# Expert stage of a decoder trunk: weight splits issued one at a time with side jobs between them, few-token experts in 64 packed columns, gates and tail reordered

## The chip, the cores and the metric

The kernel runs on one core of one Trainium2 chip. The metric is the device time of one execution in microseconds; it is taken over several executions and told as their median. TensorE is PE in the profile (its weight loads PEld), VectorE is DVE, ScalarE is ACT, SyncE is SP. SP issues the weight loads.

## The reference, cut to what matters

A trunk of layers for 256 tokens of width 1024 in float32: attention layers with dense feed-forward parts, then a mixture of eight experts, then a last RMS norm. The change touches the experts and the last norm. Each token takes two of eight experts, by the two largest router logits:

```python
logits = (xf @ router).astype(jnp.float32)
top_val, top_idx = lax.top_k(logits, TOP_K)          # TOP_K = 2
gates = jax.nn.softmax(top_val, axis=-1)
...
def swiglu(x, w_gate, w_up, w_down):
    return (jax.nn.silu(x @ w_gate) * (x @ w_up)) @ w_down
...
y_rows = lax.map(expert_block, (x_rows, blk_expert)).reshape(n_rows, dm)
y_rows = y_rows * row_gate[:, None].astype(y_rows.dtype)
y = jax.ops.segment_sum(y_rows, row_tok, num_segments=n + 1)[:n]
...
return rms_norm(x, final_norm)
```

An expert's weights are 1024 x 3584 (gate and up) and 3584 x 1024 (down), 44 MB in float32 for each of the eight.

## The kernel before

Up to about 510 us the attention and dense layers run. The expert stage follows. It has 56 **steps**: eight experts, p0 to p7 in an order by token count, times seven chunks of 512 hidden units. The arm that ran takes p0 to p4 as *few* (at most 64 tokens each, 35 steps) and p5 to p7 as *others* (up to 128 tokens, 21 steps). The two groups are interleaved by the share that each has done, so about five few steps stand beside three others. p0 ends at step 10; the last steps of p0, p5, p1, p2, p6 and p3 have their last down-product two steps later, at steps 12, 19, 23, 34, 37 and 46, inside the stream. p7 and p4 end in the tail.

**Weights.** A step needs six pieces of 128 x 2048 floats (1 MB): two of gate, two of down (for the step two earlier), two of up. SP loads them in order into a ring `raw` of `RAWS = 6` (L944). `fill` (L947) splits a piece in two: ACT copies it rounded into `wH` (L955), DVE writes the rest `wL` (L956); rings of `SPLIT = 4` each. The products use both halves.

**A step** (loop at L1272, `for s in range(n_steps + 1)`), in the order in which it is written, which is kept on PE, ACT and DVE:

- the gate products (`ffn_in`; few: 4 matmuls with `wH`, L1105, and 4 with `wL`, L1110, a piece; others 12, L1107, L1108, L1110), then `fill`, which splits all free pieces, two here;
- the copy g out of PSUM (L1124, ACT);
- `turn` for the step before: its g and u are transposed (few: multiplied with a fold matrix that adds the two halves, L1134; others: L1136); `activate` queues four operations in `later_`: silu (L1143, ACT), product (L1144, DVE), high half (L1145, ACT), low half (L1146, DVE). `fill` pops one of them after each split piece;
- `job(s)`, at most one side job or several, depending on its due step;
- the down products of the step two earlier (`ffn_out`, `y`), `fill` (two pieces), `job(s)`;
- the up products, `fill` (two pieces), the copy u (L1124, ACT).

**Side jobs.** `gather` fetches an expert's tokens by one-hot matmuls (one-hots L1069 on DVE, matmuls L1081, copies L1086 on ACT, then L1090, L1092, the copy of `rs` L1094 on DVE and of `ST` L1095 on ACT); it starts at steps 1, 3, 11, 18, 22, 33 and 36. When an expert has ended, `y_split` (L1165 ACT, L1166 DVE) splits its output and `combine` (L1174 and L1175 on PE, L1178 on DVE) adds it, scaled by the gate, into `xs` in four pieces. They are due two steps after the end and take the place at the head of `jobs`:

```python
for _ in range(min(left, max(1, -(-left // max(2 * (due - s) - 1, 1))))):
    next(j)
    next(j, None)
...
adding = [s + 2, combine(*y_split(y), gateq[:, :, p2:p2 + 1], kept[p2][1]), 4]
```

With one step left this runs all four pieces at the first `job` of the next step. PSUM banks: a ring of two `bA` (g, u, gather, combine) and of two `bT` (turn), and one `y` for each group.

At step 0 `gates()` (L1046 to L1049 and on) and `to_order()` stand ahead of the copy g. In the tail the remaining jobs run, then the activation of the last step, its last products in two halves, two combines and the last norm (L1359).

Of the kernel before, what the change touches and what calls it, by code (L numbers as in the profile page):

```python
# [8 lines left out]
F32 = mybir.dt.float32  # L9
# [3 lines left out]
AF = mybir.ActivationFunctionType  # L13
# [19 lines left out]
SPLIT = 4  # L33
HEAD = 3
# [24 lines left out]
for _n, _w in (("iota", 128), ("fold", 128)):  # L59
    CM[_n] = (_o, _o + _w)  # L60
    _o += _w
# [11 lines left out]
def trunk(tc, I, out):  # L73
    nc = tc.nc
    ctx = ExitStack()
    with ctx:
# [808 lines left out]
        with ExitStack() as ph:  # L885
# [3 lines left out]
            def few_at(a):  # L889

                i = c_m("iota")[:, 0:P // 2]
                return i[:, :, None].to_broadcast([P, P // 2, 2]) if a == 0 else i[:, None, :].to_broadcast([P, 2, P // 2])

            def c_m(n):
                return cm[:, CM[n][0]:CM[n][1]]

# [22 lines left out]
            for a in range(2):  # L919
                d = few_at(a)  # L920
# [10 lines left out]
            class Pieces:  # L931
# [14 lines left out]

                def fill(self, n=SPLIT):  # L947
                    while len(self.ready) < n:
                        self.load(1)
                        if not self.loaded:  # L950
                            break
                        raw = self.loaded.pop(0)
                        w = raw.shape[-1]
                        h, l = wHs.next()[:, :w], wLs.next()[:, :w]
                        nc.scalar.activation(h, raw, AF.Copy)  # L955
                        nc.vector.tensor_tensor(l, raw, h.bitcast(F32), op=ALU.subtract)  # L956
                        self.ready.append((h, l))
                        self.load(RAWS)
                        if later_:
                            later_.pop(0)()  # L960

                def take(self, n):
                    self.fill(n)
# [21 lines left out]
            early.fill()  # L985
# [73 lines left out]
            def onehots(pos, mode):  # L1059
# [3 lines left out]
                for a, S_ in enumerate((Sg, Ss)):  # L1063
                    at = c_m("iota") if mode is False else io[:, a, :] if mode is None else few_at(a)
                    for tt in range(NT):
                        o = S_[:, tt, :]
                        if mode:
                            o = o.rearrange("p (a b) -> p a b", a=at.shape[1])
# [3 lines left out]
            def gather(Sg, Ss, X, ST, rs, first=False):  # L1072


                for h, src in enumerate((hnH, hnL)):
                    for k0 in range(0, KD, 4):
                        pt = bank("T" if first and k0 else "A").rearrange("p (k j) -> p k j", k=4)
                        for k in range(4):
# [430 lines left out]
```

## Time and profile before

| | us |
|---|---|
| median of three runs (lowest, highest) | 1490.66 (1484.51, 1490.75) |
| the profiled execution, device time | 1486.26 |
| its span in the profile | 1484.5 |
| PE busy | 1381.8 (93%) |
| DVE busy | 1182.0 (80%) |
| ACT busy | 1033.0 (70%) |
| read from HBM | 425.61 MB, 287 GB/s over the span |

A line of the timeline reads: start, duration, engine, line of the program, operation, out<-in, form, count, and in brackets the idle time before it and what ended it. A PE matmul's duration is modelled and overlaps the next one; the distance from start to start tells what one takes. An SPq line is the queue of the loads; x2 are the two pieces of one chunk. A line of windows gives the busy time of each engine in that stretch, the granted clock of PE, the busy share of the DMA engines and the rate.

### The profile page before, as it was taken

What the parts mean: (1) busy time and instruction counts of PE and PEld (TensorE: products, weight loads), DVE (VectorE), ACT (ScalarE), POOL (GpSimd) and SP (SyncE); (2) the same over time, 40 slices, a digit from 0 to 9 for tenths busy, and PEclk for the clock granted to TensorE, in tenths of its full rate; (3) what the DMA queues carried; (4) which work ended last, traced back from release to release, by engine and by line L of the source; (5) the groups of instructions that cost most, each with busy time, mean ns of one, the idle gap of its engine ahead of it and who ended that gap; (6) DMA issues with size and microseconds to landing.
All of it is one profiled execution on the core that took longest, in us unless ns stands there. A gap on an engine that the chain in (4) does not pass through costs nothing. (4 is left out here: it accounts for less than half of the span.)

```text
span 1484.5 us, 19753 instructions
## 1 busy us (share of the span) xinstructions
PE 1381.8 (93%) x7351; PEld 1178.0 (79%) x7351; DVE 1182.0 (80%) x1255; ACT 1033.0 (70%) x1050; POOL 2.5 (0%) x12
## 2 busy tenths in 40 slices
PE   8999999999999779999899999999989899989994
PEld 7778999999887668888688777788878778868883
DVE  6847656565674578899889889799987799989995
ACT  6444444444575478898688868698867688868882
POOL 0000000000000000000000000000000000000000
PEclk9999999999999789999999999999999999989998
DMA  8435355442314378999989989799997799989990
GB/s 337 171 117 212 130 196 200 171 161 106 109 63 159 142 260 331 365 420 419 358 320 421 370 302 385 289 422 421 421 381 273 298 396 419 420 326 408 419 385 31
DMA packets 57228, 428.06 MB, mean 288 GB/s; under 512 B 6272, under 2 KB 6656, under 8 KB 10144
## 3 DMA queue, kind: packets, MB, share of 16 engines
q1 hardware_dynamic: 56784, 425.50, 73.2%
q8 instruction: 60, 0.98, 0.3%
q0 software_dynamic: 336, 1.18, 0.2%
q14 instruction: 48, 0.39, 0.1%
HBM read 425.61 MB, written 1.05 MB: 287 GB/s over the span
## 5 line engine op out<-in xcount | busy, mean ns | idle before, releaser
L956 DVE TENSOR_TENSOR wL<-raw,wH 128x2048 fp32r<-128x2048 f32 (+1 forms) x338 | 760.8, 2276 | 92.5 <-ACT wH L955 87.0
L955 ACT ACTIVATE wH<-raw 128x2048 fp32r<-128x2048 f32 (+1 forms) x338 | 634.0, 1900 | 94.9 <-PE y L1108 32.1
L147 ACT ACTIVATE wH<-raw 128x1024 fp32r<-128x1024 f32 (+3 forms) x137 | 142.4, 1042 | 167.6 <-PE pst L202 118.1
L1110 PE MATMUL bA<-wL,X 128*128 128x512 f32 x896 | 245.1, 395 | 0.0
L148 DVE TENSOR_TENSOR wL<-raw,wH 128x1024 fp32r<-128x1024 f32 (+3 forms) x137 | 164.1, 1199 | 86.9 <-ACT wH L147 78.4
L1110 PEld LDWEIGHTS bA<-wL,X 128*128 128x128 f32 x896 | 172.7, 193 | 36.3
L1105 PE MATMUL bA<-wH,X 128*128 128x512 f32 x560 | 157.1, 402 | 10.4 <-ACT g L1124 5.8
L1105 PEld LDWEIGHTS bA<-wH,X 128*128 128x128 f32 x560 | 109.2, 197 | 33.2 <-ACT g L1124 6.2
L1107 PE MATMUL bA<-wH,X 128*128 128x512 f32 x336 | 131.7, 392 | 0.3 <-ACT ST L1095 0.2
L1108 PE MATMUL bA<-wH,X 128*128 128x512 f32 x336 | 130.9, 389 | 0.0
L201 PE MATMUL pst<-hTH,wH 128*128 128x256 f32 x512 | 127.3, 286 | 0.9 <-DVE vC L743 0.5
L202 PE MATMUL pst<-hTL,wH 128*128 128x256 f32 x512 | 127.0, 285 | 0.3
L1110 PE MATMUL y<-wL,a 128*128 128x512 f32 x448 | 126.2, 404 | 0.0
L1110 PEld LDWEIGHTS y<-wL,a 128*128 128x128 f32 x448 | 88.7, 198 | 18.9
L201 PEld LDWEIGHTS pst<-hTH,wH 128*128 128x128 f32 x512 | 98.8, 193 | 2.3 <-DVE vC L743 0.9
L202 PEld LDWEIGHTS pst<-hTL,wH 128*128 128x128 f32 x512 | 99.0, 193 | 0.9 <-DVE hTL L249 0.7
L1105 PE MATMUL y<-wH,a 128*128 128x512 f32 x280 | 84.0, 422 | 6.5 <-DVE a L1146 5.0
L1108 PE MATMUL y<-wH,a 128*128 128x512 f32 x168 | 68.4, 407 | 7.7 <-DVE a L1146 7.7
L1107 PEld LDWEIGHTS bA<-wH,X 128*128 128x128 f32 x336 | 63.1, 188 | 14.2 <-ACT ST L1095 1.2
L1108 PEld LDWEIGHTS bA<-wH,X 128*128 128x128 f32 x336 | 63.1, 188 | 13.0
L204 PE MATMUL pst<-hTH,wL 128*128 128x256 f32 x512 | 72.7, 284 | 0.0
L1105 PEld LDWEIGHTS y<-wH,a 128*128 128x128 f32 x280 | 55.3, 207 | 18.1 <-DVE a L1146 6.2
(290 smaller groups left out, 1815.6 us busy)
## 6 DMA issues: line engine op xcount, KB each, us to landing
raw<-in_m_g SPq DMA_DIRECT2D x112, 1024.0 KB, 7.7
raw<-in_m_u SPq DMA_DIRECT2D x112, 1024.0 KB, 7.3
raw<-in_m_d SPq DMA_DIRECT2D x110, 1024.0 KB, 7.4
raw<-in_f_gu SPq DMA_DIRECT2D x14, 2048.0 KB, 8.5
raw<-in_f_d SPq DMA_DIRECT2D x7, 2048.0 KB, 8.4
raw<-in_w_eo SPq DMA_DIRECT2D x2, 2048.0 KB, 8.4
raw<-in_w_oo SPq DMA_DIRECT2D x2, 2048.0 KB, 7.9
raw<-in_w_qa SPq DMA_DIRECT2D x4, 512.0 KB, 7.6
```

Source lines behind the costliest of these rows:

```text
L147: nc.scalar.activation(h[:, :w], src, AF.Copy)
L148: nc.vector.tensor_tensor(l[:, :w], src, h[:, :w].bitcast(F32), op=ALU.subtract)
L201: ins.append(nc.tensor.matmul(o, a[0], b[0], start=st, stop=False))
L202: ins.append(nc.tensor.matmul(o, a[w], b[1 - w], start=False, stop=False))
L204: ins.append(nc.tensor.matmul(o, a[1 - w], b[w], start=False, stop=sp))
L955: nc.scalar.activation(h, raw, AF.Copy)
L956: nc.vector.tensor_tensor(l, raw, h.bitcast(F32), op=ALU.subtract)
L1105: nc.tensor.matmul(o, both(x), b[0], start=st, stop=False)
L1107: nc.tensor.matmul(o, x[:, 0], b[0], start=st, stop=False)
L1108: nc.tensor.matmul(o, x[:, 1], b[0], start=False, stop=False)
L1110: nc.tensor.matmul(o, both(x) if few_ else x[:, 0], b[1], start=False, stop=sp)
```

## The change

- **Splits singly.** `fill` splits one piece. It is called six times a step, twice after each pair of pieces, with other work between. It takes a function `first` that is run on DVE between the ACT copy and the DVE subtraction. Each `fill` pops one queued activation operation, also when nothing was split; the list has an empty place before the high half.
- **Order of a step.** `turn` and its job now stand behind the gate products, then fill, the copy g, fill; behind the down products a job, fill, `y_split`, fill; behind the up products fill, the copy u, fill. A side job's matmuls are issued at the job, its copy on ACT later, its addition on DVE ahead of the next subtraction (`first`).
- **Combine** is due three steps after the end: one piece, two pieces and one piece at three successive places instead of four at one. `y_split` is one operation of 1024 columns on each engine instead of two of 512.
- **Few tokens in 64 columns.** For p1 to p4 the high and low parts stand side by side in 64 + 64 columns (p0 keeps them interleaved). The fold matrix has 64 columns, the silu, product, high and low operate on 128 x 4 x 64, both transposed halves share one `bT` bank, and a gather has three jobs with two copies instead of five jobs with four copies.
- The copy of `rs` moves from DVE to ACT. `to_order()` moves behind step 0's fills, `gates()` and the ordering of the gates to step 3; `pick` and `picked` get tiles of their own.
- **Tail.** The activation of the last step stands ahead of the down products of the step before; p7's combine stands between the two halves of the last products; the multiplication with the last norm's gain stands ahead of the mean square's root, and the last scaling is split between DVE and ACT.

```diff
-                def fill(self, n=SPLIT):
+                def fill(self, first=None):
+                    if len(self.ready) < SPLIT:
...
                         nc.scalar.activation(h, raw, AF.Copy)
+                            if first is not None:
+                                first()
+                                first = None
                         nc.vector.tensor_tensor(l, raw, h.bitcast(F32), op=ALU.subtract)
...
+                    if first is not None:
+                        first()
+                    if later_:
+                        later_.pop(0)()
...
+                w, n = (HALF, KD) if few_ else (P, 4)
...
+                                nc.tensor.matmul(pt[:, k], src[:, tt, c], Sg[:, tt, 0:w], start=tt == 0, stop=tt == 1)
                         yield
+                        o = X[:, :, 0, h * HALF:(h + 1) * HALF] if few_ else X[:, k0:k0 + n, h, :]
...
-                nc.vector.tensor_copy(rs, pt[:, S:S + 1])
+                nc.scalar.activation(rs, pt[:, S:S + 1], AF.Copy)
...
+                if few_:
+                    tp = bank("T").rearrange("p (a f j) -> p a f j", a=2, f=4)
+                    tps = [tp[:, 0], tp[:, 1]]
...
+                if few_:
+                    s, hi, lo = s[:, :, 0:HALF], a[:, :, 0, 0:HALF], a[:, :, 0, HALF:P]
                 later_.extend((
                     lambda: nc.scalar.activation(s, tps[0], AF.Silu),
                     lambda: nc.vector.tensor_tensor(s, s, tps[1], op=ALU.mult),
+                    lambda: None,
+                    lambda: nc.scalar.activation(hi, s, AF.Copy),
+                    lambda: nc.vector.tensor_tensor(lo, s, hi.bitcast(F32), op=ALU.subtract)))
...
-                def job(s):
+                def job(s, more=False):
+                    due, j, left, dve = jobs[0]
+                    for i in range(min(left, max(1, -(-left // max(due - s, 1)))) if more else 1):
+                        if i > 0:
                             next(j, None)
+                        next(j)
+                        jobs[0][2] -= 1
...
+                    return (copy, None) if dve else (None, copy)
...
-                        if s == 0:
-                            gates()
-                            to_order()
-                        g = scaled(pt, rs, "g")
...
+                    on_dve, on_act = job(s)
+                    ws.fill(on_dve)
+                    g = scaled(pt, rs, "g")
+                    if on_act is not None:
+                        on_act()
+                    ws.fill()
+                    if s == 0:
+                        to_order()
+                    if s == 3:
+                        gates()
+                        in_order(gateq, gate)
...
                         ffn_out(p2 in A, ws, held.pop(("a", s - 2)), y, c2 == 0, c2 == NC - 1)
...
-                        adding = [s + 2, combine(*y_split(y), gateq[:, :, p2:p2 + 1], kept[p2][1]), 4]
+                        on_dve, on_act = job(s, True)
+                        ws.fill(on_dve)
+                        if c2 == NC - 1:
+                            adding = [s + 3, combine(*y_split(y), gateq[:, :, p2:p2 + 1], kept[p2][1]), 4, True]
+                            jobs.insert(0, adding)
+                        if on_act is not None:
+                            on_act()
+                        ws.fill()
+                    pt = ffn_in(mode, ws, X)
+                    ws.fill()
+                    held[s] = (g, scaled(pt, rs, "u"))
+                    ws.fill()
...
-                for j in jobs:
-                    run(j[1])
+                few_ = steps[-1][0] in A
                 settle()
+                a = activate(few_, turn(few_, held.pop(n_steps - 1)))
+                settle()
...
+                ffn_out(p2 in A, ws, held.pop(("a", n_steps - 2)), y, c2 == 0, c2 == NC - 1)
...
+                    for j in jobs:
+                        run(j)
+                    jobs.clear()
+                    parts = y_split(y, slice(n, n + 1), yy)
...
+                for tt in range(NT):
+                    nc.vector.tensor_tensor(of[:, tt, :], xs[:, tt, :], gf, op=ALU.mult)
                 last_rstd()
...
-                        nc.vector.scalar_tensor_tensor(of[:, tt, c], xs[:, tt, c], fr[:, tt:tt + 1], gf[:, c],
-                                                       op0=ALU.mult, op1=ALU.mult)
+                        if tt:
+                            nc.scalar.activation(of[:, tt, c], of[:, tt, c], AF.Copy, scale=fr[:, tt:tt + 1])
+                        else:
+                            nc.vector.tensor_scalar(of[:, tt, c], of[:, tt, c], fr[:, tt:tt + 1], None, op0=ALU.mult)
```

The first end of an expert in the arm that ran is p0's. On DVE, before, from the low half at step 12 on (L956 the split, L1178 the pieces of combine, L1144 the product, L1146 the low half, here of another step):

```order
L1146 TENSOR_TENSOR a_4840<-s_4838,a_4840 128x4x128
L956 TENSOR_TENSOR wL_4829<-raw_4817,wH_4825 128x2048
L956 TENSOR_TENSOR wL_4830<-raw_4818,wH_4826 128x2048
L1178 SCALAR_TENSOR_TENSOR xs<-bA_4832,gateq,xs 128x512
L1178 SCALAR_TENSOR_TENSOR xs<-bA_4831,gateq,xs 128x512
L1178 SCALAR_TENSOR_TENSOR xs<-bA_4832,gateq,xs 128x512
L1178 SCALAR_TENSOR_TENSOR xs<-bA_4831,gateq,xs 128x512
L956 TENSOR_TENSOR wL_4827<-raw_4819,wH_4823 128x2048
L956 TENSOR_TENSOR wL_4828<-raw_4820,wH_4824 128x2048
L1144 TENSOR_TENSOR s_4838<-s_4838,bT_4834 128x512
```

And now at the same place (L957 the split, L1188 the pieces, L1156 the product, L1159 the low half):

```order
L1188 SCALAR_TENSOR_TENSOR xs<-bA_4832,gateq,xs 128x512
L957 TENSOR_TENSOR wL_4829<-raw_4817,wH_4825 128x2048
L957 TENSOR_TENSOR wL_4830<-raw_4818,wH_4826 128x2048
L1156 TENSOR_TENSOR s_4838<-s_4838,bT_4834 128x4x64
L1188 SCALAR_TENSOR_TENSOR xs<-bA_4831,gateq,xs 128x512
L1188 SCALAR_TENSOR_TENSOR xs<-bA_4832,gateq,xs 128x512
L957 TENSOR_TENSOR wL_4827<-raw_4819,wH_4823 128x2048
L957 TENSOR_TENSOR wL_4828<-raw_4820,wH_4824 128x2048
L957 TENSOR_TENSOR wL_4829<-raw_4821,wH_4825 128x2048
L1159 TENSOR_TENSOR a_4839<-s_4838,a_4839 128x4x64
L957 TENSOR_TENSOR wL_4830<-raw_4822,wH_4826 128x2048
L1188 SCALAR_TENSOR_TENSOR xs<-bA_4831,gateq,xs 128x512
```

The four additions stood in one row behind two splits; now they stand one, two and one, each ahead of a split, with six splits, the product and a low half between the first and the last.

On ACT, a step of a few expert without a side job, before (L955 the copy of the split, L1124 the copies g and u, L1143 silu, L1145 the high half):

```order
L955 ACTIVATE wH_4823<-raw_4817 128x2048
L955 ACTIVATE wH_4824<-raw_4818 128x2048
L1124 ACTIVATE g_4835<-bA_4832,rs_4852 128x512
L955 ACTIVATE wH_4825<-raw_4819 128x2048
L1143 ACTIVATE s_4838<-bT_4833 128x512
L955 ACTIVATE wH_4826<-raw_4820 128x2048
L955 ACTIVATE wH_4823<-raw_4821 128x2048
L1145 ACTIVATE a_4840<-s_4838 128x4x128
L955 ACTIVATE wH_4824<-raw_4822 128x2048
L1124 ACTIVATE u_4837<-bA_4831,rs_4852 128x512
```

And now (L953 the copy of the split, L1129 g and u, L1155 silu, L1158 the high half):

```order
L953 ACTIVATE wH_4825<-raw_4817 128x2048
L1155 ACTIVATE s_4838<-bT_4834 128x4x64
L1129 ACTIVATE g_4836<-bA_4831,rs_4853 128x512
L953 ACTIVATE wH_4826<-raw_4818 128x2048
L953 ACTIVATE wH_4823<-raw_4819 128x2048
L953 ACTIVATE wH_4824<-raw_4820 128x2048
L1158 ACTIVATE a_4839<-s_4838 128x4x64
L953 ACTIVATE wH_4825<-raw_4821 128x2048
L1129 ACTIVATE u_4837<-bA_4831,rs_4853 128x512
L953 ACTIVATE wH_4826<-raw_4822 128x2048
```

The copy g stood behind two copies of the split; now it stands behind one of them and the silu, and the copy u stands between two copies of the split as before, with the high half two copies ahead of it.

## Rows read from the trace of the kernel before

**Rows 1.** The queue of the weight loads, the issues of the down pieces of a step (start, duration of the issue): an early pair, the sixth pair after it, two with six steps between them in an even stretch, and the 47th pair after the second row.

```profile
522.19 2.53 SPq L944 DMA_DIRECT2D raw<-in_m_d  x2
...
633.27 2.99 SPq L944 DMA_DIRECT2D raw<-in_m_d  x2
...
1201.69 2.93 SPq L944 DMA_DIRECT2D raw<-in_m_d  x2
...
1291.50 2.93 SPq L944 DMA_DIRECT2D raw<-in_m_d  x2
...
1421.13 2.93 SPq L944 DMA_DIRECT2D raw<-in_m_d  x2
```

**Rows 2.** Busy time of PE, PEld, DVE, ACT, POOL, then PE's granted clock, DMA share and GB/s, in 40 us around p0's end and in 40 us of the even stretch.

```profile
720.00:760.00 40.00, 34.19 (x156) 27.55 (x155) 31.16 (x23) 26.29 (x24) 0.00 (x0) 0.91 0.80 297
1240.00:1280.00 40.00, 39.03 (x190) 32.81 (x189) 38.86 (x23) 34.90 (x27) 0.00 (x0) 1.00 1.01 419
```

**Rows 3.** DVE by line from 633.27 to 1421.13 us: operation and form, count, busy us, mean ns of one, idle time before them and what ended it.

```profile
L956 DVE TENSOR_TENSOR wL<-raw,wH 128x2048 fp32r<-128x2048 f32 x282 | 637.9, 2288 | 62.8 <-ACT wH L955 58.8 <-PE bA L1105 2.2
L1146 DVE TENSOR_TENSOR a<-s,a 128x512 fp32r<-128x512 f32 x47 | 32.2, 685 | 0.0
L1144 DVE TENSOR_TENSOR s<-s,bT 128x512 f32<-128x512 f32 x47 | 32.0, 681 | 0.0
L1178 DVE SCALAR_TENSOR_TENSOR xs<-bA,gateq,xs 128x512 f32<-128x512 f32 x24 | 17.4, 747 | 4.5 <-PE bA L1175 3.9
L1166 DVE TENSOR_TENSOR yy<-y,yy 128x512 fp32r<-128x512 f32 x12 | 8.3, 688 | 4.0 <-ACT yy L1165 4.0
...
L1069 DVE TENSOR_SCALAR Sg<-cm,posq 128x128 fp32r<-128x128 f32 x10 | 2.4, 281 | 0.0
```

**Rows 4.** The timeline of PE in the even stretch: a few step's turn (L1134) and its down products, another expert's products (L1107 on), few products again, the turn of another expert (L1136) and what follows it.

```profile
1219.48 1.05 PE L1134 MATMUL bT<-cm,g 128*128 128x128 f32 x8
1220.37 1.06 PE L1134 MATMUL bT<-cm,u 128*128 128x128 f32 x8
1221.18 1.18 PE L1105 MATMUL y<-wH,a 128*128 128x512 f32 x4
...
1224.99 0.39 PE L1107 MATMUL bA<-wH,X 128*128 128x512 f32 x1
...
1230.44 1.09 PE L1105 MATMUL bA<-wH,X 128*128 128x512 f32 x4
...
1234.17 0.60 PE L1136 MATMUL bT<-cf,g 128*128 128x128 f32 x4
...
1234.98 1.20 PE L1105 MATMUL y<-wH,a 128*128 128x512 f32 x4
```

**Rows 5.** The timeline of PE's weight loads: of a gather (128 columns moved), of the product with one column (L1092), of a fold (128 columns).

```profile
593.09 1.09 PEld L1081 LDWEIGHTS bA<-Sg,hnL 128*128 128x128 f32 x8
...
744.55 0.52 PEld L1092 LDWEIGHTS bA<-ry,Ss 128*128 128x128 f32 x4
...
755.50 0.97 PEld L1134 LDWEIGHTS bT<-cm,u 128*128 128x128 f32 x8
```

**Rows 6.** The timeline at p0's end: DVE's splits, the first combine pieces on PE, and the first split of the next pair.

```profile
731.37 4.48 DVE L956 TENSOR_TENSOR wL<-raw,wH 128x2048 fp32r<-128x2048 f32 x2
...
733.33 0.80 PE L1174 MATMUL bA<-yy,ST 128*128 128x512 f32 x1 [2.55 <-ACT g L1124]
...
736.57 0.79 PE L1174 MATMUL bA<-yy,ST 128*128 128x512 f32 x1 [2.02 <-DVE xs L1178]
...
741.00 1.92 ACT L955 ACTIVATE wH<-raw 128x2048 fp32r<-128x2048 f32 x1 [7.73 <-PE y L1108]
...
742.95 2.29 DVE L956 TENSOR_TENSOR wL<-raw,wH 128x2048 fp32r<-128x2048 f32 x1 [3.52 <-ACT wH L955]
```

**Rows 7.** Stretches of 4 us at and after this end, columns as in the windows above.

```profile
732.00:736.00 4.00, 1.22 (x2) 0.50 (x2) 4.00 (x3) 1.27 (x2) 0.00 (x0) 0.59 1.01 401
740.00:744.00 4.00, 4.00 (x20) 3.29 (x19) 1.05 (x1) 2.62 (x3) 0.00 (x0) 1.00 0.28 115
772.00:776.00 4.00, 4.00 (x18) 3.30 (x18) 4.00 (x3) 4.00 (x5) 0.00 (x0) 1.00 1.01 426
```

**Rows 8.** Waits from 560 to 1460 us: who waits for whom, us in total, times, longest.

```profile
DVE wL L956 <- ACT wH L955: 73.5, 89, 4.6
ACT a L1145 <- DVE s L1144: 44.3, 38, 2.6
```

**Rows 9.** The timeline at step 0: the copy g and the products behind it.

```profile
528.12 0.69 ACT L1124 ACTIVATE g<-bA,rs 128x512 f32<-128x512 f32 x1 [2.42 <-DVE u L1207]
...
528.87 2.08 PE L1105 MATMUL bA<-wH,X 128*128 128x512 f32 x4 [5.81 <-ACT g L1124]
```

**Rows 10.** The timeline of the tail: the last up products, the fold behind the copy u, the down products of the step before the last, the first of the last products, the last norm.

```profile
1446.05 1.09 PE L1110 MATMUL bA<-wL,X 128*128 128x512 f32 x4
...
1450.99 1.16 PE L1134 MATMUL bT<-cm,u 128*128 128x128 f32 x8 [2.96 <-ACT u L1124]
...
1456.72 1.07 PE L1110 MATMUL y<-wL,a 128*128 128x512 f32 x4
...
1464.81 0.73 PE L1105 MATMUL y<-wH,a 128*128 128x512 f32 x2 [1.50 <-DVE a L1146]
...
1478.19 2.74 DVE L1359 SCALAR_TENSOR_TENSOR raw<-xs,fr,gf 128x512 f32<-128x512 f32 x4
```

More of the change, by code (lines that the diff above doesn't have):

```diff
@@ L33 @@
 SPLIT = 4
+HALF = 64
 HEAD = 3
@@ L58 @@
 _o = 0
-for _n, _w in (("iota", 128), ("fold", 128)):
+for _n, _w in (("iota", 128), ("fold", 64)):
     CM[_n] = (_o, _o + _w)
@@ L918, in trunk @@
             io = ss.bufs[0][:, 0:2, :]
-            for a in range(2):
-                d = few_at(a)
+            for a, d in enumerate((half[:, :, None].to_broadcast([P, HALF, 2]), twice)):
                 n = d.shape[1]
@@ L984, in trunk @@
             early.load(RAWS)
-            early.fill()
+            for _ in range(SPLIT):
+                early.fill()
             top = mw.tile([P, NT, 8], F32, name="top")
@@ L1150, in ffn_out, with y_split @@
                 for j, w in enumerate(ws.take(2)):
[L1151 removed]
+                    products([(y[:, n, :], a[:, 2 * j + f], part(w, 2 * f + n), first and j + f == 0,
                                last and j + f == 2) for f in range(2) for n in range(2)], few_)
[L1153 removed]
             ys = []
             for i in range(2):
[L1157 to L1160 removed]
+                ys.append(pa.tile([P, 2, 512], F32, name=f"y{i}"))
+            def y_split(y, n=slice(0, 2), yy=None):
                 if yy is None:
@@ L1314, in experts @@
                     for j, w in enumerate(ws.take(2)):
-                        products([(y[n], a[:, 2 * j + f], part(w, f), False, j + f == 2) for f in range(2)], p in A)
-                    ws.fill()
-                    parts = y_split(y, (n,), yy)
+                        products([(y[:, n, :], a[:, 2 * j + f], part(w, f), False, j + f == 2) for f in range(2)], few_)
+                        ws.fill()
+                    for j in jobs:
+                        run(j)
+                    jobs.clear()
+                    parts = y_split(y, slice(n, n + 1), yy)
                 for n in range(2):
@@ L1351, in overflow @@
                             squares(n)
+                        for tt in range(NT):
+                            nc.vector.tensor_tensor(of[:, tt, :], xs[:, tt, :], gf, op=ALU.mult)
                         last_rstd()
+            of = raws.bufs[0].rearrange("p (t c) -> p t c", t=NT)
             def final_norm():
-                of = raws.next().rearrange("p (t c) -> p t c", t=NT)
                 for tt in range(NT):
```

132 lines of the change are left out of this document (59 added, 73 removed).

## The prediction, made before the changed kernel ran

> **What bounds the kernel now.** I read the queue of the weight loads first, because every step of the expert stage needs the same six megabytes. In an even stretch six steps take 1291.50 − 1201.69 = 89.81 us, 14.97 a step [rows 1], and the windows there show the DMA engines fully busy at 419 GB/s [rows 2]. From 633.27 to 1421.13 us, 47 steps, the queue needs 787.86 us, 16.76 a step; at the even pace it would be 47 x 14.97 = 703.6. So 84.3 us are lost on the way, and the six ends of experts lie in this stretch: 14.0 each. The first six steps of the queue take 633.27 − 522.19 = 111.08, which is 21.3 over the even pace.
>
> Then I ask how near the other engines are to the same bound, since what the stream could give back they may not take. DVE: its six largest groups in the 787.86 us add to 637.9 + 32.2 + 32.0 + 17.4 + 8.3 + 2.4 = 730.2 us [rows 3], that is 26.6 over the stream's floor. PE, from start to start [rows 4]: a pair of pieces of a few expert takes 1234.17 − 1230.44 = 3.73, its turn 1221.18 − 1219.48 = 1.70, so a few step 3 x 3.73 + 1.70 = 12.89. Another expert's pair takes 1230.44 − 1224.99 = 5.45, its turn 0.81, so its step 17.16. Mixed five to three this is 14.49. To that come five gathers of 32 matmuls at (1.09 − 0.19) / 7 = 0.13 [rows 5] and six small ones at 0.11, 4.8 each, and six combines of 8 x 0.23 = 1.9: 47 x 14.49 + 24 + 11 = 716. The three floors are 704, 716 and 730, and the time is 788. The gap that an end's stalls can explain is therefore 58 us with DVE's work as it is, not 84.
>
> Where the 58 go is seen at p0's end. All four combine pieces stand in a row: PE waits 2.55 us for ACT's copy g, which stands behind two splits, and 2.02 for DVE's addition [rows 6]. PE's products come late, so the ring of four splits is not freed: ACT's next copy has been idle for 7.73, DVE for 3.52, and the clock of PE is granted at 0.59 in 732 to 736, the DMA engines fall to a share of 0.28 in 740 to 744 [rows 7]. Afterwards nothing can catch up: the rate at 772 to 776 is 426 GB/s [rows 7], hardly over the 419 of the even stretch. Of DVE's waits for ACT there are 73.5 us in all [rows 8].
>
> **Splits singly, combine spread, copies ahead of the second split.** The order on DVE shows one, two and one additions instead of four in a row, and on ACT the copy g behind one split copy and not two. PE's wait of 2.55 for g (one split copy is 1.92 [rows 6]) falls to about 0.6, its wait of 2.02 for the addition goes where one piece stands alone, since at least two splits, 4.48 us [rows 6], lie between two places, and stays at most once, where two pieces stand together. A piece's addition stands ahead of a split, so DVE can now wait there for PE: at most the product behind the turn, 1.70 + 0.46. I keep 2.5 us an end for these, between 0 and 10. New instructions: none; the place where nothing is split but an operation is popped costs nothing that I can see.
>
> **Half-width activations.** Two DVE operations of each few step (0.681 and 0.685) shrink from 512 to 256 elements. The trace has 0.281 for 128 and 0.681 for 512 [rows 3]; the line through them gives 0.415 for 256. Of 47 steps 29 are few: 29 x 2 x 0.267 = 15.5 us, which brings DVE's floor from 730 to 715. In the even stretch this moves nothing, for there the stream is the limit at 38.86 of 40 us of DVE [rows 2]. Its worth is that an end's own work (4 x 0.747 + 2 x 0.688 + the one-hots) finds room. The narrower fold and gather matmuls I cost at nothing: four loads for a product with one column take 0.52 us [rows 5], (0.52 − 0.19) / 3 = 0.11 each; eight for a fold with 128 columns take 0.97, (0.97 − 0.19) / 7 = 0.11 each. The load sets the pace, and the loads stay as they are. If the columns did, half of 0.11 on 16 folds in 29 steps and 32 matmuls in four gathers would take 25.5 + 7 = 33 us from PE's floor.
>
> The Trainium skill, page "TensorE: Matmul & The Clock Gate", section "Back-to-back issue gap", gives 134 cycles for 128 columns and about 60 for 64, 31 ns less for each. By it the same 592 matmuls would save an estimated 18 us of PE, which would put its floor under the stream's and the time at rival two's. No run so far has 64 columns; the rows on one column speak against it, and the sum goes by them.
>
> **The stage's sum.** PE's floor is still 716, DVE's now 715, the stream's 704. They can't all be met, as PE's need is uneven: I let a backlog grow step by step by PE's need less 14.97, never below zero, and count what exceeds 5 us (two pieces of the ring) as lost. That gives 17 us over the stage, with 10 us of room 12; I take 15, so 719. With 2.5 us at six ends it is 734, against 788: **−54**. With ends free and more room it is 716, −72; with 10 us left at each end 704 + 60, −24. The copy of `rs` on ACT, `y_split` in one operation (saves one overhead in 0.688) and the shared bank go with this term.
>
> **Startup.** At step 0 the copy g waits behind the gates and PE stands 5.81 us [rows 9]. The gates move to step 3, where 1 to 2 us of small operations stand between splits. **−6**, from −12 (more of the 21.3 us) to 0 (the wait comes back at step 3, since DVE has no slack).
>
> **Tail.** From the last up product, 1446.05, to the end of the span at 1484.5 there are 38.4 us. PE waits 2.96 for the copy u [rows 10], which now stands one split copy further ahead: about 2 gone. The last products start at 1464.81, about 7.2 us after the down products before them were through (1456.72 + 0.93), because the activation comes after them in program order; now it comes first. I credit 4 of the 7.2, as p7's combine now stands in between. The last norm's 2.74 us [rows 10] are split over two engines, but the multiplication is added ahead: nothing. **−6**, from −9 to −2.
>
> **The sum.** −54 − 6 − 6 = −66 against the profiled execution's 1486.26 (span 1484.5 and 1.8 around it): **1420**. The median of the three runs, 1490.66, is 4.4 above that execution; against the median it is −71. All bounds together give 1393 and 1460.
>
> **Rivals.** *One: the stalls form again.* DVE waits ahead of each of three splits for a combine product that PE issues only after products and turn, and the two-piece place waits as before. For it: in the even stretch DVE has 1.14 us in 40 free [rows 2], so any wait is paid in full. Against it: three places of 2 us are less than the 7.73 of one. Price: about 8 us left at an end instead of 2.5, 33 more: 1453 (1438 to 1475).
>
> *Two: PE's narrower matmuls are faster.* Then PE's floor falls to 716 − 33 = 683, PE runs ahead of the stream nearly everywhere, the backlog of 15 and the 15 of the ends vanish with it, and DVE sets 715: 73 less instead of 54, 1401 (1390 to 1406). For it: no row has 64 columns. Against it: the rows on one column.
>
> *Three: slower.* The silu now stands right behind the first split copy on ACT, ahead of copy g and the second split. It needs PE's turn, which comes only after the gate products. If ACT waits there for the turn in each step, all of it stands: ACT is busy 34.90 of 40 us [rows 2], 13.06 of 14.97, so it has 1.9 us a step. A wait of 1.70 (the turn) less 1.92 (the split copy ahead of it) is nothing, and the wait of 44.3 us in 38 cases for the product [rows 8] gets room. It decides only from a wait of about 2.2 us a step; at 4 us a step 2 us x 50 would show, 1420 + 100 = 1520.
>
> *Four: no change.* The loss at an end comes from the work itself, not from its clumping, since DVE and PE have little room in any order; the stalls only spread: 1483 to 1491.
>
> **How the numbers follow.** Forecast (1406 to 1437) 0.60, rival one 0.16, rival two 0.14, rival three 0.05, rival four 0.05. A measurement tells about 0.5% apart, 7.4 us here. Faster by more than that are the forecast and the first two rivals: 0.90; same 0.05; slower 0.05. The range leaves out rivals three and four, the upper part of rival one and the lower end of two, 0.2 in all: 1393 to 1458.
>
> **What would show it.** In the profile after: the down pieces of the queue 47 steps apart by about 734 us instead of 788; DVE's groups in that stretch at about 715; no stretch at an end with a DMA share below 0.6 and no wait of PE over 2 us for copy g; the product L1156 at about 0.415; eight loads of a fold still in 0.97; the last products about 4 us sooner after the last up product. Wrong it would be if PE's folds space at 0.06, if DVE's idle time ahead of its splits stays near 60 us in the 47 steps, or if ACT's silu shows a wait of over 2 us in most steps.

## The result and the profile after

The changed kernel takes 1441.96 us in the median of four runs (1428.50 to 1453.91), the kernel before 1489.28; the ratio is 0.9601, 95% interval 0.9562 to 0.9639. Measured a second time (r1 below) it is 0.9656 (0.9604 to 0.9709). In some executions of most of these kernels 20 to 30 us are lost ahead of the expert stage at a lower granted clock of PE (0.56 instead of 1.00 from 80 to 120 us), the first profile of the changed kernel and those of r4, r8, r10 and r12 among them; the ratios leave most of these out (r3's holds one, r10's three), and the rows of after come from a second profiled execution of the same kernel, r1, 1426.91 us with a span of 1425.1. Against the profiled 1486.26 of before that is −59.4; forecast were −66, to 1420, within 1393 to 1458.

I compare by the expert stage itself: from its first one-hot on DVE to the end of the span. It takes 984.1 us before and 924.8 after (928.2 in the first profile: about 3 us between two executions of one kernel). The queue of the weight loads divides it, issues of the down pieces as in [rows 1]: the first pair, the sixth after it, the 53rd after it.

```profile
520.10 4.26 SPq L942 DMA_DIRECT2D raw<-in_m_d  x2
...
624.20 4.06 SPq L942 DMA_DIRECT2D raw<-in_m_d  x2
...
1361.72 2.87 SPq L942 DMA_DIRECT2D raw<-in_m_d  x2
```

The first six steps take 104.1 us instead of 111.1, the 47 steps 737.5 instead of 787.9, and from there to the end 63.4, as before. The first pair comes 19.8 us behind the first one-hot instead of 21.8. So the gain is 50.3 in the 47 steps, 9 at the start, nothing in the tail.

Where in the 47 steps, the distances from pair to pair tell. An end of an expert before shows as one long step, 24.7, 24.2, 25.1, 26.3, 24.0 and 21.7 us at the 12th, 19th, 23rd, 34th, 37th and 46th pair. After, these are 16.1, 16.7, 16.1, 16.8, 17.9 and 16.1. With the step behind each, the twelve take 235.1 before and 195.8 after: 39 of the 50 us. Windows of 40 us around p0's end, beside [rows 2]:

```profile
700.00:740.00 40.00, 38.78 (x198) 32.34 (x197) 36.47 (x25) 33.84 (x29) 0.00 (x0) 1.00 0.97 371
```

PE is busy 38.78 instead of 34.19, at full clock instead of 0.91, and the DMA share is 0.97 instead of 0.80. Of the windows of 4 us in the 47 steps one has a DMA share below 0.6, against 13 before. DVE by line over the 47 steps, beside [rows 3]:

```profile
L957 DVE TENSOR_TENSOR wL<-raw,wH 128x2048 fp32r<-128x2048 f32 x282 | 633.2, 2284 | 36.2 <-ACT wH L953 36.1
L1159 DVE TENSOR_TENSOR a<-s,a 128x256 fp32r<-128x256 f32 (+1 forms) x48 | 24.8, 516 | 0.0
L1156 DVE TENSOR_TENSOR s<-s,bT 128x256 f32<-128x256 f32 (+1 forms) x47 | 24.2, 515 | 0.0
L1188 DVE SCALAR_TENSOR_TENSOR xs<-bA,gateq,xs 128x512 f32<-128x512 f32 x24 | 17.4, 746 | 7.9 <-PE bA L1185 7.5
L1176 DVE TENSOR_TENSOR yy<-y,yy 128x1024 fp32r<-128x1024 f32 x6 | 7.3, 1219 | 0.4 <-ACT yy L1175 0.4
...
L1074 DVE TENSOR_SCALAR Sg<-cm,posq 128x64 fp32r<-128x64 f32 (+1 forms) x10 | 2.2, 260 | 0.0
```

The product and the low half fell from 64.2 to 49.0 us (the rows mix both widths; at 256 elements the product takes 0.413 us, forecast 0.415), the six groups from 730.2 to 709.1; the idle time ahead of the splits fell from 62.8 to 36.2. The timeline at p0's end, beside [rows 6], PE's first combine piece, the addition, the splits behind it, the next two additions, the up products and the last addition:

```profile
718.56 0.47 PE L1184 MATMUL bA<-yy,ST 128*128 128x512 f32 x1
...
720.67 0.74 DVE L1188 SCALAR_TENSOR_TENSOR xs<-bA,gateq,xs 128x512 f32<-128x512 f32 x1
...
721.34 4.48 DVE L957 TENSOR_TENSOR wL<-raw,wH 128x2048 fp32r<-128x2048 f32 x2
...
726.07 1.40 DVE L1188 SCALAR_TENSOR_TENSOR xs<-bA,gateq,xs 128x512 f32<-128x512 f32 x2
...
726.87 1.21 PE L1111 MATMUL bA<-wH,X 128*128 128x512 f32 x4 [1.22 <-DVE xs L1188]
...
738.55 0.75 DVE L1188 SCALAR_TENSOR_TENSOR xs<-bA,gateq,xs 128x512 f32<-128x512 f32 x1 [1.95 <-PE bA L1185]
```

Nothing waits for the copy g any more. What is left is PE's 1.22 for the pair of additions, and DVE's 1.95 for the product ahead of the last one. Both are the waits that I had put down as left.

### The profile page after: what moved, and what is told of

It reads as the page before. It is cut to its first block, busy times and chain, and to the rows that moved or that the text cites. A ratio compares the mean times of both kernels' runs of the same rounds, so it can differ in the third digit from the quotient of the medians.

```text
span 1449.7 us, 19640 instructions
## 1 busy us (share of the span) xinstructions
PE 1382.4 (95%) x7351; PEld 1179.1 (81%) x7351; DVE 1154.8 (80%) x1240; ACT 1020.5 (70%) x1046; POOL 2.5 (0%) x12
## 5 line engine op out<-in xcount | busy, mean ns | idle before, releaser
L957 DVE TENSOR_TENSOR wL<-raw,wH 128x2048 fp32r<-128x2048 f32 (+1 forms) x338 | 756.1, 2272 | 58.8 <-ACT wH L953 58.3
L953 ACT ACTIVATE wH<-raw 128x2048 fp32r<-128x2048 f32 (+1 forms) x338 | 635.4, 1907 | 51.0 <-DMA raw<-in_m_g 10.7
L1116 PEld LDWEIGHTS bA<-wL,X 128*128 128x128 f32 x896 | 169.4, 190 | 41.7 <-DVE wL L957 6.3
L1111 PE MATMUL y<-wH,a 128*128 128x512 f32 x280 | 81.0, 411 | 1.4 <-DVE yy L1176 1.4
L1113 PE MATMUL y<-wH,a 128*128 128x512 f32 x168 | 69.4, 413 | 0.0
L1114 PE MATMUL y<-wH,a 128*128 128x512 f32 x168 | 68.1, 405 | 1.0 <-DVE a L1159 1.0
```

Of the source, the lines that this page charges most:

```text
L1111: nc.tensor.matmul(o, both(x), b[0], start=st, stop=False)
L1113: nc.tensor.matmul(o, x[:, 0], b[0], start=st, stop=False)
L1114: nc.tensor.matmul(o, x[:, 1], b[0], start=False, stop=False)
L1116: nc.tensor.matmul(o, both(x) if few_ else x[:, 0], b[1], start=False, stop=sp)
```

## Experiments

All are made from the changed kernel unless it is said; "stage", "first six", "47 steps" and "tail" are the stretches above in one profiled execution, "ends" the twelve steps, in us.

| | stage | first six | 47 steps | ends | tail | ratio (95%) |
|---|---|---|---|---|---|---|
| before | 984.1 | 111.1 | 787.9 | 235.1 | 63.4 | 1 |
| r1 again | 924.8 | 104.1 | 737.5 | 195.8 | 63.4 | 0.9656 (0.9604–0.9709) |
| r2 four in a row, ahead | 929.1 | 104.4 | 742.2 | 200.0 | 62.9 | 0.9785 (0.9718–0.9853) |
| r3 one at four places | 916.6 | 104.2 | 729.0 | 188.7 | 63.7 | 0.9600 (0.9511–0.9688) |
| r4 full width on DVE | 940.7 | 105.6 | 751.4 | 201.9 | 63.3 | 0.9740 (0.9687–0.9792) |
| r5 old schedule | 955.1 | 104.9 | 764.6 | 223.5 | 65.9 | 0.9821 (0.9785–0.9858) |
| r6 gates at step 0 | 933.9 | 106.5 | 743.3 | 197.2 | 64.2 | 0.9680 (0.9639–0.9721) |
| r7 copy g behind both | 923.2 | 105.5 | 735.5 | 198.2 | 62.4 | 0.9609 (0.9585–0.9633) |
| r8 r3, other tail | 914.2 | 102.6 | 726.9 | 188.8 | 64.7 | 0.9568 (0.9542–0.9593) |
| r9 1-2-1, behind splits | 962.7 | 106.6 | 773.3 | 234.7 | 62.9 | 0.9893 (0.9850–0.9936) |
| r10 four, behind splits | 964.3 | 106.5 | 773.8 | 237.2 | 64.0 | 0.9941 (0.9880–1.0003) |
| r11 r3, gather copies later | 911.8 | 102.9 | 725.8 | 189.8 | 63.4 | 0.9495 (0.9429–0.9561) |
| r12 before, combine ahead | 969.6 | 111.1 | 768.0 | 209.7 | 68.8 | none, see r12 |

Two profiles of the same work differ by 3.4 us in the stage (r1 and the first profile of the changed kernel; r3 and r8 up to the tail), but by 0.1 in the ends.

**r1.** No edit. 

> The changed kernel once more, unaltered, as the base for the others and to see where its first profile lost 21 us ahead of the expert stage. Theory: the stage, from its first one-hot to the end of the span, takes 928 us again (984 before), whatever the span is. Rival: the 21 us belong to the change, and the span is 1449 again.

924.8: the 21 us were not the change's.

**r2.** The combine's four pieces behind the down products, all at once.

```diff
+                    if dve and not more:
+                        return None, None
...
-                            adding = [s + 3, combine(
+                            adding = [s + 2, combine(
```

> The four combine pieces of an end in a row at one place, behind the next step's down products, instead of one, two and one at three places. Theory (the spread is what saves the ends): 3 to 6 us are lost again at each of six ends, the stage takes 946 to 964 instead of 928. Rival (single splits and the order of the copies do it, whatever the spread): 925 to 933.

929.1, 4.3 over r1, 4.2 of it at the ends. My theory that the spread over three places saves the ends falls: in a row, at a good place, the four cost 4 us in all.

**r3.** Only the due step.

```diff
-                            adding = [s + 3, combine(
+                            adding = [s + 4, combine(
```

> The combine due one step later, so that it stands one piece at each of four places. Theory (what is left at an end is PE's wait for the addition where two pieces stand together, 8 us on up products and 2 on combine products in the trace): the stage takes 920 to 926 instead of 928. Rival (the bank and DVE's waits only move to another place): 926 to 932.

916.6, 8.2 less and a little more than expected, 7.1 of it at the ends; the place with two pieces was the last wait of PE for additions at an end. From r2 to r3, four in a row to four places, it is 12.5.

**r4.** The two DVE operations of few steps at 512 elements.

```diff
-                    tp = bank("T").rearrange("p (a f j) -> p a f j", a=2, f=4)
+                    tp = bank("T").rearrange("p (f a j) -> p f a j", a=2, f=4)
...
+                        lambda: nc.vector.tensor_tensor(whole, whole, tps[2], op=ALU.mult),
...
+                        lambda: nc.vector.tensor_tensor(all_[:, :, 1:3], whole.rearrange("p f (b j) -> p f b j", b=2), all_[:, :, 0:4:3].bitcast(F32), op=ALU.subtract)))
```

> On DVE the product and the low half of few steps operate on 512 elements again, of which 256 are of no use; all else stays packed. DVE gets 35 x 2 x 0.27 = 19 us more work, 15.5 of them in the 47 steps. Theory (DVE's floor would be 730 there, about the time that the stage now takes): 8 to 18 us longer, the stage 936 to 946. Rival (DVE has room for it, half-width brings nothing): 926 to 931.

940.7, 15.9 over r1 and 13.9 of it in the 47 steps, of which the ends have 6.1. DVE's work is on the path, outside the ends too.

**r5.** The step written as before: both splits, then copy g, turn, jobs with their copies at once; likewise behind the other products. In this version p4's shorter gather is through before p6's combine and overwrites its scatter matrix, so p6's rows go to wrong tokens; the amount of work is the same.

```diff
                     pt = ffn_in(mode, ws, X)
-                    if s >= 1:
...
-                    on_dve, on_act = job(s)
-                    ws.fill(on_dve)
+                    ws.fill()
+                    ws.fill()
                     g = scaled(pt, rs, "g")
...
+                    both_jobs(s)
```

> The changed kernel with the step's old schedule: two splits behind each pair of products, copy g behind both, turn and jobs behind that, combine in a row of four due after two steps; the packed columns with half-width operations, the gates at step 3 and the new tail stay. Theory, after the run with clumped combine gave only 4 us: the order of the step as a whole (copy g and side jobs between single splits) is worth what half-width (14 to 16) and startup (9) leave of the 59, and the stage takes 950 to 962 instead of 925. Rival: the order is worth little and the packing brings the rest by its fewer gather copies and shorter ACT operations: 928 to 940.

955.1: of the 59 us the order of the step, the place of the additions among it, holds 30.

**r6.** `gates()`, `to_order()` and the ordering of the gates moved ahead of step 0's copy g.

```diff
+                    if s == 0:
+                        gates()
+                        to_order()
+                        in_order(gateq, gate)
                     g = scaled(pt, rs, "g")
```

> The gates and their ordering at step 0 ahead of the copy g again, all else as changed. Theory (PE's wait of 5.8 us behind the gates was on the path): the queue's first stretch of six steps, with what lies ahead of it, takes 5 to 9 us longer, the stage 930 to 934 instead of 925. Rival (the wait was covered by the weights' arrival): 924 to 927.

933.9, 9 more as the theory has it, but not where it has it. The first six steps lose 2.4. The other 5.8 of the 47 steps come later, 3.2 of them at one step, where ACT waits for a gather's product:

```profile
809.62 0.60 ACT L1093 ACTIVATE X<-bA 128x512 fp32r<-128x512 f32 x1 [3.90 <-PE bA L1087]
```

At most the 2.4 can be put down to the gates: the first profile of the changed kernel has 740.8 in the 47 steps, only 2.6 less than r6.

**r7.** The copy g one line lower.

```diff
-                    g = scaled(pt, rs, "g")
-                    if on_act is not None:
-                        on_act()
                     ws.fill()
+                    g = scaled(pt, rs, "g")
+                    if on_act is not None:
+                        on_act()
```

> Only the copy g behind both splits of its place instead of one. Theory (PE waits for g's bank and for the turn's next products when a side job stands behind it): 4 to 12 us longer, the stage 929 to 937 instead of 925. Rival (down products of 3.7 to 5.5 us lie between and hide it): 923 to 927.

923.2, within what two executions differ by. The place of the copy g, taken alone, is worth nothing.

**r8.** On r3, p7's combine behind both halves of the last products.

```diff
-                yy, p = yys.next(), steps[-1][0]
+                yy, p = kept[p2][0].rearrange("p k h j -> p (k h j)"), steps[-1][0]
...
-                    for j in jobs:
-                        run(j)
-                    jobs.clear()
                     parts = y_split(y, slice(n, n + 1), yy)
+                for j in jobs:
+                    run(j)
+                jobs.clear()
```

> The version with one piece at each of four places, and in the tail p7's combine behind both halves of the last products, with a buffer of its own for p4's output halves. Theory (in the changed tail the last products wait for DVE's additions of p7's combine, 2.0 and 1.4 us): the tail, from the 47th pair's issue to the end, takes 60 to 61.5 us instead of 63.4 to 63.7. Rival (DVE's additions set the end in any order): 63 to 64.

The tail takes 64.7; the theory's 60 to 61.5 is missed, and the rival's 63 to 64 is exceeded.

**r9.** Pieces one, two and one, but each job and its addition behind the two splits of its place.

```diff
-                    on_dve, on_act = job(s)
-                    ws.fill(on_dve)
+                    ws.fill()
                     g = scaled(pt, rs, "g")
-                    if on_act is not None:
-                        on_act()
                     ws.fill()
+                    for f in job(s):
+                        if f is not None:
+                            f()
```

and the same behind the down products. 

> The changed kernel with one, two and one combine pieces as it has them, but all side jobs and their additions issued behind the two splits of their place instead of ahead of the next split; the copy g stays between the splits. Theory (the old step's 30 us come from four additions that stand in a row behind two splits, while PE holds its two banks; either half of it, spread or ahead, is enough): the stage takes 925 to 933. Rival (the place ahead of the split alone is what counts): 940 to 952.

962.7: my theory falls again, the rival's 940 to 952 is even exceeded. The ends take 234.7, as before the change. Its timeline at p0's end: the addition of the first piece, two splits, the next two additions, the up products and ACT's next split copy:

```profile
727.88 0.75 DVE L1188 SCALAR_TENSOR_TENSOR xs<-bA,gateq,xs 128x512 f32<-128x512 f32 x1
728.54 4.49 DVE L957 TENSOR_TENSOR wL<-raw,wH 128x2048 fp32r<-128x2048 f32 x2
...
732.94 1.41 DVE L1188 SCALAR_TENSOR_TENSOR xs<-bA,gateq,xs 128x512 f32<-128x512 f32 x2
...
733.74 2.07 PE L1111 MATMUL bA<-wH,X 128*128 128x512 f32 x4 [4.33 <-DVE xs L1188]
...
735.90 1.91 ACT L953 ACTIVATE wH<-raw 128x2048 fp32r<-128x2048 f32 x1 [7.02 <-issue]
```

Windows of 4 us there, and PE's waits for additions from 560 to 1420 us:

```profile
728.00:732.00 4.00, 0.73 (x2) 0.30 (x2) 4.00 (x3) 0.88 (x2) 0.00 (x0) 1.00 1.00 406
732.00:736.00 4.00, 2.26 (x5) 1.82 (x6) 2.35 (x3) 0.10 (x1) 0.00 (x0) 0.60 1.02 422
736.00:740.00 4.00, 4.00 (x11) 3.11 (x10) 2.16 (x1) 1.81 (x1) 0.00 (x0) 0.55 0.70 293
```

```profile
PE bA L1111 <- DVE xs L1188: 20.7, 6, 4.3
PE bA L1113 <- DVE xs L1188: 10.1, 3, 4.3
PE bA L1184 <- DVE xs L1188: 8.9, 5, 3.2
```

In r1 the same waits, from 560 to 1390 us, are

```profile
PE bA L1111 <- DVE xs L1188: 7.8, 4, 3.5
...
PE bA L1113 <- DVE xs L1188: 2.1, 2, 1.7
```

The circle is to be seen here. PE needs a bank of the ring of two, which the addition holds; the addition stands behind two splits, 4.49 us; PE waits 4.33 and uses up no weights meanwhile, ACT's split copies stand idle for 7.02 us (the profile names no releaser; the buffers that PE has not freed are my reading), and PE resumes at a granted clock of 0.60 and 0.55.

Of the 39.7 us of these waits 26.0 are six times 4.33, for the products behind two pieces that hold both banks. Another 8.9 are the second of the two pieces, which waits for the addition of the single piece before it, and 4.8 the products behind the last, single piece, at three of the six ends, p0's among them:

```profile
753.02 0.75 DVE L1188 SCALAR_TENSOR_TENSOR xs<-bA,gateq,xs 128x512 f32<-128x512 f32 x1
...
753.82 0.50 PE L1113 MATMUL bA<-wH,X 128*128 128x512 f32 x1 [1.49 <-DVE xs L1188]
```

One piece at each of four places, behind the splits, was not run.

**r10.** r9 with all four pieces in a row straight behind the turn, due after two steps, and five buffers for `ST` instead of four.

```diff
+                    for i in range(left if dve else min(left, max(1, -(-left // max(due - s, 1)))) if more else 1):
...
-            STs, rss = Ring(mw, "ST", 4, [P, NT, P], F32R), Ring(mw, "rs", 4, [P, 1])
+            STs, rss = Ring(mw, "ST", 5, [P, NT, P], F32R), Ring(mw, "rs", 4, [P, 1])
```

> The same, and all four combine pieces in a row straight behind the turn, as the kernel before has them; one more buffer for the scatter matrices keeps p6's. Theory (both together: clumped and behind the splits): near the old schedule's 955, 947 to 957, with steps of 21 to 24 us at the six ends. Rival (the rest of the old order, silu and turn behind copy g, makes the 30 us): 925 to 938.

964.3, ends 237.2, over the theory's 947 to 957 and far over the rival's. Behind the splits, one, two and one or in a row makes next to no difference (r9), ahead of them 4 us (r2).

**r11.** On r3, a gather's copies on ACT behind the second split copy.

```diff
+                    ws.fill()
                     if on_act is not None:
                         on_act()
-                    ws.fill()
```

> The version with one piece at each of four places, and a gather's copies on ACT behind the second split copy of their place instead of ahead of it. Theory (ACT waits 14 to 18 us in all for PE's gather products there, and the split copy behind it and DVE wait too): 4 to 9 us less, the stage 907 to 913 instead of 916.6. Rival (PE has no idle time left there but 11 us in the whole stage, so ACT's wait is not on the path): 915 to 919.

911.8, 4.8 less than r3, inside the theory's 4 to 9. ACT's wait for gather products falls from 17.6 us to 1.4. What that is worth is not clear of noise: r8 has r3's stream and took 726.9 for the 47 steps where r3 took 729.0 and r11 725.8. r11 has the lowest ratio, 0.9495, with an interval that overlaps r8's; the stage is 13 us under that of the changed kernel.

**r12.** The kernel before with one part of the change: the combine pieces, still in a row, behind the down products and ahead of that place's splits.

```diff
+                    ahead = adding[2] > 0
+                    if not ahead:
+                        job(s)
...
+                    if ahead:
+                        job(s)
+                    if s >= 2:
+                        ws.fill()
```

> The kernel before, with one part of the change alone: at an end the four combine pieces stay in a row, but behind the down products and with their additions ahead of that place's two splits; nothing else is altered, two splits at a time and full-width operations stay. Theory, from the two runs with the additions behind the splits: the place in DVE's queue is what the ends cost, so each of six ends gives back 4 to 6 us and the stage takes 948 to 962 instead of 984; the steps at the ends take 18 to 20 instead of 22 to 26. Rival (single splits and the spread are needed as well): 972 to 985.

969.6, between theory and rival. No ratio is given, as a single execution, 1469.88 us, is left to time it by. The long steps fall to 19.2, 17.7, 19.2, 19.2, 17.7 and 17.7, the ends by 25.4 and the 47 steps by 19.9, but the tail takes 5.4 longer, with PE at a granted clock of 0.50 from 1466 to 1478 us (before the change 1.00 from 1446 to 1474 us). PE's waits for additions from 560 to 1440 us are all but gone:

```profile
PE bA L1173 <- DVE xs L1177: 2.4, 6, 0.4
...
PE bA L1105 <- DVE xs L1177: 0.8, 4, 0.2
```

## Why the prediction was right, and where not

**The bound and the size.** The forecast of −54 for the 47 steps measured −50.3, and no version contradicts the floors of 704, 716 and 715: none went under 725.8 (r11). DVE's groups came to 709.1, a little under the 715. Reading only the queue would have promised 84. The bound of −24 is reckoned from the stream's 704; from the 719 that the sum uses it would be −9. The 15 us of backlog in the 719 were not taken apart by any run. That the total came within 7 us, −59.4 for −66, owes something to luck: the startup gave 3 us more than forecast, for another reason, and the tail 6 less.

**The ends: right place, wrong term.** "Splits singly, combine spread, copies ahead of the second split" put the loss on four pieces in a row and on the copy g, and gave the place of an addition ahead of a split no worth, only a risk ("so DVE can now wait there for PE"). That is the step that failed: the term that it had at nothing carries most. In r9 the pieces are spread as in the changed kernel, the copy g stands between the splits and PE's order is the same; only the additions stand behind two splits, and with them the gathers' copies, which by r11 cost nothing there, and an end's `y_split`, for which PE does not wait in r9. The stage loses 38 us, and the ends cost 234.7 as before. The spread is worth 4 us over three places (r2) and 12 over four (r3), where the additions stand ahead of a split. That "its wait of 2.02 for the addition goes where one piece stands alone" holds ahead of a split: with one piece at each place (r3) PE has no wait for additions left. Behind two splits it fails: in r9 13.7 us of PE's waits hang on the addition of a single piece.

I had read the wait for g [rows 6] as a cause by itself. The copy g alone is worth nothing (r7), and where it moves ahead while four additions stay behind the splits (r10), PE waits less for g and more for the additions, 34.7 us in all instead of 28.7. Before, from 560 to 1460 us, and r10, from 560 to 1420 us:

```profile
PE bA L1174 <- ACT g L1124: 14.9, 6, 3.1
PE bA L1174 <- DVE xs L1178: 13.8, 6, 2.5
...
PE bA L1184 <- DVE xs L1188: 29.1, 6, 5.8
PE bA L1184 <- ACT g L1129: 5.6, 6, 2.2
```

r12 is the counter-test in the kernel before: with the additions ahead of the splits, in a row, two splits at a time and full width, the ends give back 25.4 us and the 47 steps 19.9 of the 50.3. It moves the pieces on PE too, behind the down products, where g has long been copied, so it does not divide the wait for the additions from the wait for g; r9 and r10 do.

**Half width** was sized right, 15.5 for the 47 steps against 13.9 (r4), and so was its reason, DVE's floor; that it would tell only at the ends was not, as 7.8 of the 13.9 lie outside them. The fold's 64 columns bring nothing, as forecast; the weight loads after, beside [rows 5]:

```profile
717.64 0.97 PEld L1143 LDWEIGHTS bT<-cm,u 128*128 128x128 f32 x8
```

Eight loads take 0.97 us again, (0.97 − 0.19) / 7 = 0.11 each, so rival two is out. The Trainium skill, page "TensorE: Matmul & The Clock Gate", section "Back-to-back issue gap", has about 60 cycles for 64 columns and 134 for 128, as the isolated gap of a matmul; it says itself that in a stream of weight loads and matmuls both set the spacing. This trace shows no such difference for these matmuls. The same page's section "LDWEIGHTS (loading the stationary operand)" gives P / 1.2 ns, for 128 columns an estimated 107 ns, and with that the 0.11 agrees.

**Startup**, −6 forecast, −9 measured (2.0 ahead of the first pair, 7.0 behind it), but not for the reason forecast. In r6 the gates stand ahead of the copy g again and PE's 5.81 does not come back: the next products start without a wait, and the first six steps take 2.4 longer, where those of r3 and r8, which are the same, differ by 1.6. What the copy g had waited for [rows 9] is the ordering on DVE, which before used the buffers of g and u as scratch and now has tiles of its own. First two rows from before, then r6:

```profile
526.83 0.23 DVE L1216 TENSOR_TENSOR g<-by,cm 128x64 f32<-128x64 f32 x1
...
527.74 0.29 DVE L1207 TENSOR_TENSOR u<-gate,g 128x128 f32<-128x128 f32 x1
```

```profile
520.84 0.67 ACT L1129 ACTIVATE g<-bA,rs 128x512 f32<-128x512 f32 x1
...
522.19 1.09 PE L1111 MATMUL bA<-wH,X 128*128 128x512 f32 x4
522.32 0.29 DVE L1217 TENSOR_TENSOR picked<-posp,pick 128x128 f32<-128x128 f32 x1
```

In r6 the copy g no longer waits for the ordering, which runs after it. No run has the tiles alone, so that they hold the rest is my reading; r4 gives back 1.5 in the first six, and the gathers' shorter jobs and the copy of `rs` on ACT remain as candidates too.

**Tail**, −6 forecast, 0.0 measured. The second term came: from the last up product's start to the first of the last products there were 1464.81 − 1446.05 = 18.8 us [rows 10], now 1398.13 − 1384.46 = 13.7, and the 7.2 us that lay between the down products and the last products are gone. Three steps failed. The wait for the copy u, "about 2 gone", is 2.28 where it was 2.96. p7's combine, for which 3.2 of the 7.2 were kept back, takes 4.7 between the halves: the second half starts 1406.43 − 1398.13 = 8.3 us behind the first, before 1468.42 − 1464.81 = 3.6. And from there to the end 18.7 us pass instead of 16.1, which the forecast had at nothing. Now:

```profile
1384.46 1.19 PE L1116 MATMUL bA<-wL,X 128*128 128x512 f32 x4 [0.19 <-DVE wL L957]
...
1388.77 1.10 PE L1143 MATMUL bT<-cm,u 128*128 128x64 f32 x8 [2.28 <-ACT u L1129]
...
1398.13 0.62 PE L1111 MATMUL y<-wH,a 128*128 128x512 f32 x2
...
1403.60 0.50 PE L1184 MATMUL bA<-yy,ST 128*128 128x512 f32 x1 [1.96 <-DVE xs L1188]
...
1406.43 1.22 PE L1111 MATMUL y<-wH,a 128*128 128x512 f32 x2 [1.44 <-DVE yy L1176]
...
1410.01 0.63 PE L1184 MATMUL bA<-yy,ST 128*128 128x512 f32 x1
...
1414.12 2.35 DVE L1363 TENSOR_TENSOR raw<-xs,gf 128x1024 f32<-128x1024 f32 x2
...
1416.39 0.15 DVE L1204 TENSOR_TENSOR sst<-fss 128x2 f32<-128x2 f32 x1
```

and before:

```profile
1468.42 0.74 PE L1105 MATMUL y<-wH,a 128*128 128x512 f32 x2 [1.47 <-DVE yy L1166]
...
1470.39 0.39 PE L1174 MATMUL bA<-yy,ST 128*128 128x512 f32 x1
```

The products of the second half take 1410.01 − 1406.43 = 3.6 us instead of 1470.39 − 1468.42 = 2.0. The granted clock is 0.52 there, in 1408 to 1412 us, and was 1.00 in 1466 to 1470 before; why it falls now is open. The sum of squares on DVE (L1204) starts 2.2 us behind the last addition instead of 1.1, since the multiplication with the gain stands between them. So 40.6 us remain from the last up product to the end, 38.4 before, and the tail comes out even only because that product starts 2.2 us sooner after the 47th pair. r8 moved the combine behind both halves and gained nothing; its down products ran at a granted clock of 0.66 and its last products at 0.50.

**The rivals.** One, stalls formed again ahead of the splits, is out: DVE's additions wait 7.5 us for PE in all, and the two-piece place, which it names, cost 8 us and not 33 (r3). By the median alone, 1441.96, it could not be told from the forecast: that lies in rival one's range (1438 to 1475), not in the forecast's own (1406 to 1437). The 47 steps tell, 737.5 us where the forecast has 734 and rival one, with 33 more, 767. Three is out: of ACT's waits from 560 to 1405 us in r1 this is the one on the turn, 1.6 us each in 21 cases, under the 2.2 from which it would decide. Four is out.

```profile
ACT s L1155 <- PE bT L1143: 32.9, 21, 2.9
```

## What to carry to other kernels

A small operation that frees a buffer for a busy engine belongs ahead of the long operations in its queue; here its place was worth 38 us (r9), and spreading it over three places 4, over four 12. Before a wait is blamed, move the one instruction alone: the wait for g, which I had read as a cause in [rows 6], was a passenger, and the one at step 0 seems to have hung on a shared buffer, not on the order. And where a stage runs near the limit of three engines, sum each of them: the smallest gap bounds the gain.

## What the runs showed that I had not expected

Pairs of the queue come 14.1 us apart in many steps after the change, which would be 6.29 MB in 14.14 us or 445 GB/s. The windows of r1 show less, at most 426 in 14 us and 422 in 40 us. My reading is that the issue runs ahead of the transfer for a step and falls back in the next (16.5, 14.1, 14.1, 15.3). So one distance between issues is no rate; over 47 steps it is.
